# A transformer block's MLP on one core: the early pairs' evictions, splits and row steps set one sum apart

## The chip, the cores and the metric

The kernel runs on one core of a Trainium2 chip. The metric is the device time of one execution in microseconds. A core has five engines that work at once, each through its own queue in order: TensorE (PE, matrix products, into banks of PSUM), VectorE (DVE), ScalarE (ACT), GpSimd (POOL) and SyncE (SP, which here only starts transfers). SP, ACT and POOL each start DMA transfers from their queues. An engine goes on until an instruction waits for another engine's result.

## The reference, cut to what matters

One layer of a diffusion backbone: a token mixer (pooling and neighbourhood attention, one output projection), then a squared-ReLU MLP, each between two RMS norms with modulation. All tensors are 32-bit floats; 1024 tokens, width 1024, hidden width 4096. What the change touches is the end of the mixer and the start of the MLP:

```python
def _rmsnorm(x, g):
    y = x32 * lax.rsqrt(jnp.mean(x32 * x32, axis=-1, keepdims=True) + EPS)
    return (y * g.astype(jnp.float32)).astype(x.dtype)
def _modulate(x, gain, shift, scale):
    return _rmsnorm(x, gain) * (1 + scale) + shift
def _sq_relu_mlp(h, w1, w2):
    return jnp.square(jax.nn.relu(h @ w1)) @ w2
...
x = x + gt1 * _rmsnorm(mix_x, g_post_mix[l])
y_x = _sq_relu_mlp(_modulate(x, g_pre_mlp[l], sh2, sc2), w_mlp_in[l], w_mlp_out[l])
x = x + gt2 * _rmsnorm(y_x, g_post_mlp[l])
```

## The kernel before, in words

**Products.** A 32-bit product is made of three products of rounded parts: each operand is split into a high part (a copy cast to the rounded type, by ScalarE) and a low part (the operand less its high part, by VectorE), and `three` (lines 173 to 175) adds high × high, high × low and low × high. Large products are made by a scheme of seven products in place of eight: each operand is cut into four blocks, and sums of blocks are multiplied. In the MLP's first product the weights' blocks are A11, A12, A22 and the combinations S1 to S4; the tokens' blocks are B11, B21, B22 and the combinations T1 to T4. B11 and B21 come from the first 512 tokens alone.

**Pairs.** The 4096 hidden features are 16 pairs p of 256. A pair needs seven **sums**; a sum is 12 matmuls of 128 × 128 by 128 × 512 (four blocks of the inner dimension, three products each) in one PSUM bank. The first sum (A11 by B11) is copied out as s1 (`first_sum`, line 1329), the second (A12 by B21) goes on in the same bank phx and gives, with Relu and square, the hidden block r11 (`second_sum`, `squared`, lines 1276 and 1277), which is kept in DRAM (hdA11). The other five (S2 by T2 in bank phy, S1 by T1 and S4 by B22 in phz, S3 by T3 and A22 by T4 in phv) are made in `block_pair`.

**The early pairs.** The first two sums of a pair need only the first half of the tokens. So while the second half of the tokens is still on its way through the residual, the norms and the transposes, TensorE makes the first two sums of pairs 0 to EARLY − 1 (8). s1 of the first SPILLED pairs (4) goes to DRAM and is loaded again (`reload`); r11 of all early pairs is loaded again too.

**The row steps** (`row_steps`), one chain for each of the rows t = 4 to 7 (128 tokens each): `gate_steps` (ScalarE's mean square, jo; VectorE's product with the gate into mp1), `row_root` (vm on VectorE, a power on POOL, rm), `row_added` (VectorE adds the residual into xr, POOL's queue stores it as x1, ScalarE takes its mean square, sx), `row_second` (vn on VectorE, a power on POOL, rn), `row_scaled` (VectorE, into mp1). When all four are there, 32 transposes (px) and ScalarE and VectorE make the second token half (nf), `second_steps` makes T1 and T2 on VectorE and T3 and T4 by adding transfers from POOL's queue (`add_to`), and `token_part` splits ten pages (th the high, tl the low part).

**What sets the order.** Around the change the order on ScalarE and VectorE is the program's own: `in_order` ties every instruction of these engines to the one before it, from `last_product` to the end of the early pairs; TensorE's order is the program's from the projection on. After that, in pairs 1 to 14, a scheduler places VectorE's and ScalarE's work. Each call of `step` first makes the weight parts of the sum that comes four sums later (`more`: cast and subtraction, wpA11_p and wpA12_p), then the sum's matmuls. Loads of weights (wa) go through SP's queue into four buffers. The early loop is

```python
for q in both:
    xs[q], early[q] = first_sum(q)
    if q != 3:
        next(between)
for q in both:
    second_sum(q, xs[q])
    next(between, None)
```

where `between` goes through the row steps and then the second half's steps, one piece at a time.

## Time and profile before

| | us |
|---|---|
| median of 3 runs | 1062.57 |
| lowest, highest | 1061.94, 1064.35 |
| the profiled execution | 1062.89 |
| its span, first to last instruction | 1061.1 |
| mean granted TensorE clock in it | 0.992 |

A row of the time-ordered view has the start and length in us, the engine, the line of the kernel, the operation, output and inputs by the program's names without numbers, the shapes, how many equal instructions follow each other, and in brackets how long the engine was idle before it and whose result ended that. A view of waits has total, number and longest. A view by stretches has the busy time of each engine with the number of its instructions in parentheses, then the clock that TensorE was granted (1.00 is full), the mean busy share of the DMA engines and the rate.

### The profile page before, as it was taken

How to read it: one execution, taken by the hardware profiler on the slowest of the kernel's cores; microseconds unless marked ns; L12 is line 12 of the kernel's file. 1: busy time of each engine (PE TensorE's matmuls, PEld its weight loads, DVE VectorE, ACT ScalarE, POOL GpSimd, SP SyncE). 2: the span in 40 equal slices, each digit the busy share in tenths (PEclk: the TensorE clock that was granted, in tenths of full speed). 3: DMA queues.
4: the chain of work that ended last, by engine and by line, in shares of the span. 5: the costliest groups of instructions: out<-in, count | busy, mean ns of one | idle time of the engine just before them, and what ended most of it. 6: DMA issues, size and time to landing. Idle time of an engine off the chain costs nothing.

```text
span 1061.1 us, 15511 instructions
## 1 busy us (share of the span) xinstructions
PE 1037.5 (98%) x5878; PEld 853.6 (80%) x5878; DVE 709.6 (67%) x1115; ACT 531.9 (50%) x925; POOL 91.5 (9%) x145
## 2 busy tenths in 40 slices
PE   8999999999999999889999999999999999999997
PEld 7788888877888788677888888888888888888885
DVE  5535736537997598668988766665577566557586
ACT  7562021257888556766555455554563335334441
POOL 2020000051321302410000000000000000000001
PEclk9999999999999999898999999999999999999999
DMA  9905854023337776675766445345597666546556
GB/s 344 323 21 197 281 178 128 21 74 99 71 91 190 165 187 196 216 173 175 259 216 218 149 138 189 129 152 196 207 358 261 235 238 220 192 165 202 176 188 206
DMA packets 104891, 196.97 MB, mean 186 GB/s; under 512 B 8048, under 2 KB 42608, under 8 KB 104816
## 3 DMA queue, kind: packets, MB, share of 16 engines
q1 hardware_dynamic: 81888, 150.82, 43.4%
q10 hardware_dynamic: 16848, 30.44, 7.7%
q0 software_dynamic: 6080, 14.71, 6.5%
q8 instruction: 46, 0.75, 0.3%
q14 instruction: 29, 0.24, 0.1%
HBM read 147.70 MB, written 38.81 MB: 176 GB/s over the span
## 4 chain that ended last, share of the span: by engine, by line
PE 92%; ACT 4%; DVE 2%; issue 1%; DMA 1%; SPq 0%; ACTq 0%; POOL 0%; DVEq 0%; POOLq 0%
PE pk L409 4%; PE S L723 3%; PE pa L799 3%; PE pyv L174 3%; PE pyv L173 3%; PE pyz L174 3%; PE pyz L173 3%; PE pyx L174 3%; PE phv L175 3%; PE phz L175 3%; PE pyx L175 3%; PE phz L173 3%; PE phv L173 3%; PE phv L174 3%; PE phz L174 3%; PE pyx L173 3%
## 5 line engine op out<-in xcount | busy, mean ns | idle before, releaser
L173 PE MATMUL phx<-thB,wpA 128*128 128x512 f32 x128 | 52.8, 413 | 10.5 <-ACT s L1329 10.5
L1276 ACT ACTIVATE c<-c 128x512 f32<-128x512 f32 x48 | 30.3, 632 | 53.7 <-DVE c L1381 22.5
L746 ACT ACTIVATE sp<-sp,nm 128x640 f32<-128x640 f32 (+1 forms) x64 | 51.4, 803 | 9.0 <-DVE nm L737 8.7
L140 POOL TENSOR_TENSOR ry<-vy,nhalf 128x1 f32<-128x1 f32 x8 | 4.4, 549 | 584.5 <-DVE vy L138 584.5
L737 DVE CUSTOM_DVE_ANT_0 sp<-S,tab 128x640 f32<-128x640 f32 (+1 forms) x56 | 42.8, 802 | 17.9 <-PE S L723 11.4
L145 DVE TENSOR_TENSOR wpS<-S,wpS 128x512 fp32r<-128x512 f32 x64 | 43.8, 687 | 13.0 <-ACT wpS L144 13.0
L174 PE MATMUL phx<-tlB,wpA 128*128 128x512 f32 x128 | 51.9, 406 | 0.0
L175 PE MATMUL phx<-thB,wpA 128*128 128x512 f32 x128 | 51.7, 404 | 0.0
L144 ACT CAST wpS<-S 128x512 fp32r<-128x512 f32 x64 | 39.3, 615 | 23.6 <-PE phv L175 9.2
L173 PEld LDWEIGHTS phx<-thB,wpA 128*128 128x128 f32 x128 | 25.4, 198 | 17.0 <-ACT s L1329 11.8
L1277 ACT ACTIVATE c<-c 128x512 f32<-128x512 f32 x48 | 30.3, 631 | 12.8 <-DVE sa L1344 12.1
L175 PEld LDWEIGHTS phx<-thB,wpA 128*128 128x128 f32 x128 | 25.3, 198 | 5.6
L174 PEld LDWEIGHTS phx<-tlB,wpA 128*128 128x128 f32 x128 | 25.5, 199 | 5.3
L723 PE MATMUL S<-kT,q 64*128 64x384 f32 (+1 forms) x128 | 27.9, 495 | 0.4 <-DVE nm L737 0.4
L1389 DVE TENSOR_TENSOR c<-u,phz 128x512 f32<-128x512 f32 x16 | 11.0, 686 | 25.0 <-PE phz L175 25.0
L799 PE MATMUL pa<-pt,v 128*64 128x128 f32 x352 | 25.9, 280 | 0.8 <-ACT px L779 0.3
L784 DVE COPY pt<-T 128x512 f32<-128x512 f32 x32 | 21.9, 686 | 5.4 <-PE T L765 5.4
L173 PE MATMUL phy<-thT,wpS 128*128 128x512 f32 x64 | 24.9, 389 | 0.0
L174 PE MATMUL phy<-tlT,wpS 128*128 128x512 f32 x64 | 24.9, 389 | 0.0
L175 PE MATMUL phy<-thT,wpS 128*128 128x512 f32 x64 | 24.9, 389 | 0.0
L173 PE MATMUL phz<-thT,wpS 128*128 128x512 f32 x64 | 24.9, 389 | 0.0
L174 PE MATMUL phz<-tlT,wpS 128*128 128x512 f32 x64 | 24.9, 389 | 0.0
(1024 smaller groups left out, 3340.9 us busy)
## 6 DMA issues: line engine op xcount, KB each, us to landing
b<-in_w SPq DMA_DIRECT2D x64, 512.0 KB, 4.2
hrS<-hdS SPq DMA_DIRECT2D x32, 512.0 KB, 5.3
hrA<-hdA SPq DMA_DIRECT2D x24, 512.0 KB, 5.6
wm<-in_w_mod SPq DMA_DIRECT2D x16, 512.0 KB, 9.7
wa_0w<-in_w SPq DMA_DIRECT2D x16, 512.0 KB, 5.5
wa_1w<-in_w SPq DMA_DIRECT2D x16, 512.0 KB, 4.3
hdA<-c ACTq DMA_DIRECT2D x32, 256.0 KB, 2.1
hdS<-sa ACTq DMA_DIRECT2D x32, 256.0 KB, 2.6
```

The costliest lines, as they stand in the source:

```text
L144: nc.scalar.copy(hi, src)
L145: nc.vector.tensor_tensor(lo, src, hi.bitcast(F32), sub)
L173: nc.tensor.matmul(ps, ahi, bhi, start=first, stop=False, skip_group_check=more)
L174: nc.tensor.matmul(ps, ahi, blo, start=False, stop=False, skip_group_check=more)
L175: nc.tensor.matmul(ps, alo, bhi, start=False, stop=last, skip_group_check=more)
L409: nc.tensor.matmul(pks[b][j], wk(wgt, k, low, j * P, P), r, start=(k == 0 and n == 0), stop=(k == KT - 1 and n == 2))
L723: nc.tensor.matmul(S[e][:, c0 : c0 + keys.shape[1]], q[hs, cols], keys[hs], start=True, stop=True)
L737: nc.vector.tensor_tensor_reduce(out=to, in0=s, in1=bt, scale=1.0, scalar=BIG, op0=add, op1=ALU.min, accum_out=nm)
L746: nc.scalar.activation(sp, sp, AF.Exp, bias=least[i, e], scale=-1.0, accum_out=sums[i][:, e : e + 1])
L799: nc.tensor.matmul(pa[e * HD : (e + 1) * HD, cols], v[:, f : f + HD], turns[i][:, e, c] if c < 4 else fifths[i][:, :, (e + 1) * HD : (e + ...
L1276: nc.scalar.activation(r, src, AF.Relu)
L1277: nc.scalar.activation(r, r, AF.Square)
```

## The change

The early pairs become ten (EARLY 10), and six first sums go to DRAM (SPILLED 6). The early stage is now one loop over single sums, each a step, in which things are set apart in time:

- What ends a sum (`ending`: the copy of a first sum, or Relu and square of a second) is emitted at the head of the next step, before that step's weight cast.
- Of every split in the stage ScalarE's cast is emitted in its step and VectorE's subtraction in the next (`behind`, `caught_up`).
- For pairs 0 to 3 the square after the Relu moves from ScalarE to VectorE, one step later, and the transfer that keeps it two steps later.
- The row steps are cut into ten pieces instead of six, with `row_squared` (ScalarE's mean square of the added row) split off; row 7's second-half gate steps move from before the first sum to the second step.
- The transposes of the second half stand ahead of pair 5's second sum, after eleven sums of the early stage instead of eight; each of the two T combinations and each of the ten token pages has a step of its own. What is left of them after the last sum follows in one go.

Its core (`less_split` is now a case of `step_split`):

```diff
+    def step_split(src, hi, lo, less=False):
+        if less:
+            nc.scalar.activation(hi, src, AF.Copy, scale=-1.0)
+        else:
+            nc.scalar.copy(hi, src)
+        def second():
...
+        if stepwise:
+            behind.append(second)
+        else:
+            second()
...
             nc.gpsimd.dma_start(x1d[t], xt)
+            if t < 4:
+                row_squared(t)
+
+        def row_squared(t):
             root[t] = sm(f"sx_{t}", 1, 4)
-            mean_square(mp1[t], xt, root[t])
+            mean_square(mp1[t], rows[t], root[t])
...
+        def row_steps():
+            yield
             gate_steps(1, 7)
             gate_steps(0, 4)
             yield
             row_root(4)
             gate_steps(0, 5)
+            yield
+            row_added(4)
             row_root(5)
+            yield
+            row_squared(4)
+            row_added(5)
             gate_steps(0, 6)
             yield
             row_second(4)
+            row_squared(5)
             row_root(6)
             gate_steps(0, 7)
             yield
+            row_scaled(4)
             row_second(5)
+            row_added(6)
             row_root(7)
...
-            for name, src in (("T2", t2), ("T1", t1), ("T3", b12), ("B22", b22), ("T4", b21)):
+            for kp in range(2):
+                combined(kp)
+                yield
+            for name in ("T2", "T1", "T3", "B22", "T4"):
                 for kp in range(2):
-                    token_part(name, kp, src[kp])
-                yield
+                    token_part(name, kp, source[name][kp])
+                    yield
...
-        EARLY, SPILLED = 8, 4
+        EARLY, SPILLED = 10, 6
...
+        def second_kept(p, x):
+            r11 = part(f"r11_{p}")
+            if p < 4:
+                nc.scalar.activation(r11, x, AF.Relu)
+                def square():
+                    nc.vector.tensor_tensor(r11, r11, r11, mul)
+                    behind.append(lambda: keep("A11", p, r11))
+                behind.append(square)
+            else:
+                squared(x, r11)
+                defer(keep, "A11", p, r11)
+            return r11
...
+            stepwise.append(True)
+            between, xs, ending = row_steps(), {}, None
             for p in range(0, EARLY, 2):
...
+                for sum in (1, 2):
+                    for q in (p, p + 1):
+                        if ending:
+                            ending()
+                        caught_up()
+                        if (q, sum) == (5, 2):
+                            between = second_steps(*second_half())
+                        if sum == 1:
+                            xs[q] = bank(f"phx{q}")
+                        step(xs[q], "B11" if sum == 1 else "B21", sum == 1)
+                        next(between, None)
+                        if sum == 1:
+                            ending = lambda q=q: early.update({q: first_kept(q, xs[q])})
+                        else:
+                            ending = lambda q=q: second_kept(q, xs[q])
+            ending()
+            caught_up()
+            for _ in between:
+                caught_up()
+            caught_up()
+            stepwise.clear()
```

What this does to the queues, at three places. ScalarE's queue from row 5's mean square to the copy of pair 2's first sum (s1_2 from bank phx2), before:

```order
L131 ACTIVATE mp1_5_4660,sx_5_4978<-xr5_4667 128x1024
L131 ACTIVATE jo0_7_4980,ssm0_2016<-co0_7_4853 128x512
L148 ACTIVATE wpA12_3_4983<-wa3w_4911 128x512
L1276 ACTIVATE r11_1_4998<-phx1_4910 128x512
L1277 ACTIVATE r11_1_4998<-r11_1_4998 128x512
L1297 DMA hdA11_0_4677<-r11_1_4998 128x512
L131 ACTIVATE mp1_6_4819,sx_6_5012<-xr6_4669 128x1024
L144 CAST wpA11_4_5018<-wa4w_5016 128x512
L1329 COPY s1_2_5033<-phx2_5015 128x512
```

and in the change, from pair 0's Relu (r11_0) to the same copy:

```order
L1382 ACTIVATE r11_0_4954<-phx0_4884 128x512
L157 ACTIVATE wpA12_3_4958<-wa3w_4906 128x512
L1382 ACTIVATE r11_1_4978<-phx1_4905 128x512
L1339 DMA hdA11_0_4677<-r11_0_4954 128x512
L159 CAST wpA11_4_4986<-wa4w_4984 128x512
L131 ACTIVATE mp1_4_4656,sx_4_5000<-xr4_4665 128x1024
L131 ACTIVATE jo0_6_5004,ssm0_2016<-co0_6_4817 128x512
L1369 COPY s1_2_5007<-phx2_4983 128x512
```

The copy stood behind three rows' mean squares (4 to 6); it now stands behind row 4's alone, and the two squares of r11 are gone from this queue.

VectorE's queue beside it (co is the row's mixer output, vm and vn the sums under the roots), before:

```order
L149 SCALAR_TENSOR_TENSOR wpA12_2_4949<-wa2w_4887,wpA12_2_4949 128x512
L136 TENSOR_SCALAR vn_4_4968<-sx_4_4944 128x1
L138 SCALAR_TENSOR_TENSOR vm_6_4972<-ssm0_2016,ssm1_2017 128x1
L1034 SCALAR_TENSOR_TENSOR xr5_4667<-mp1_5_4660,rm_5_4940,xr5_4667 128x1024
L1013 TENSOR_TENSOR mp1_7_4884<-co0_7_4853,Ga_3853 128x512
L149 SCALAR_TENSOR_TENSOR wpA12_3_4983<-wa3w_4911,wpA12_3_4983 128x512
```

and in the change:

```order
L163 SCALAR_TENSOR_TENSOR wpA12_2_4933<-wa2w_4885,wpA12_2_4933 128x512
L1385 TENSOR_TENSOR r11_0_4954<-r11_0_4954 128x512
L1055 SCALAR_TENSOR_TENSOR xr4_4665<-mp1_4_4656,rm_4_4949,xr4_4665 128x1024
L138 SCALAR_TENSOR_TENSOR vm_5_4974<-ssm0_2016,ssm1_2017 128x1
L163 SCALAR_TENSOR_TENSOR wpA12_3_4958<-wa3w_4906,wpA12_3_4958 128x512
L1385 TENSOR_TENSOR r11_1_4978<-r11_1_4978 128x512
```

The subtraction of pair 3's A12 stood behind row 5's residual and follows row 4's now; each Relu's square has its place after a subtraction.

ScalarE's queue at the end of the early stage, from the Relu of the last early pair to the copy of pair 0's z, before:

```order
L1276 ACTIVATE r11_7_5372<-phx7_5309 128x512
L1277 ACTIVATE r11_7_5372<-r11_7_5372 128x512
L1297 DMA hdA11_3_4680<-r11_7_5372 128x512
L148 ACTIVATE wpA22_0_5382<-wa0_1w_5279 128x512
L144 CAST wpS2_1_5407<-S2_1_5405 128x512
L1376 COPY c22_0_5422<-phz0_5398 128x512
```

and in the change:

```order
L1318 ACTIVATE r11_9_5440<-phx9_5375 128x512
L1319 ACTIVATE r11_9_5440<-r11_9_5440 128x512
L1339 DMA hdA11_4_4681<-r11_9_5440 128x512
L159 CAST thB22_1_5446<-nf1_3_5222 128x1024
L159 CAST thT4_0_5450<-nf0_2_4857 128x1024
L159 CAST thT4_1_5454<-nf0_3_4877 128x1024
L157 ACTIVATE wpA22_0_5464<-wa0_1w_5349 128x512
L1433 COPY c22_0_5504<-phz0_5480 128x512
```

Three token pages now stand after the last early sum, where none did.

## The prediction

> **What bounds the kernel now.** First the page's list of engines: TensorE is busy almost all the time, so only its idle and slow stretches are to be won.

> ```profile
> PE 1037.5 (98%) x5878; PEld 853.6 (80%) x5878; DVE 709.6 (67%) x1115; ACT 531.9 (50%) x925; POOL 91.5 (9%) x145
> ```

> Then busy time by stretches (columns: stretch and length in us, then PE, PEld, DVE, ACT, POOL busy with instruction counts, granted PE clock, DMA share, GB/s):

> ```profile
> 300.00:400.00 100.00, 99.50 (x927) 81.21 (x926) 75.71 (x167) 67.30 (x153) 17.88 (x20) 1.00 0.70 171
> 400.00:500.00 100.00, 89.51 (x401) 73.58 (x401) 74.09 (x105) 68.23 (x116) 20.44 (x24) 0.93 0.63 187
> 500.00:600.00 100.00, 100.00 (x443) 82.81 (x442) 85.97 (x137) 53.53 (x92) 0.00 (x0) 1.00 0.66 222
> 423.24:487.23 63.99, 53.50 (x227) 43.38 (x226) 44.66 (x60) 46.21 (x77) 14.70 (x16) 0.89 0.62 178
> ```

> One stretch of the three is both idle and at a lower clock, and the change is in it: 423.24 to 487.23 us is the stage of the early pairs, from the first matmul of pair 0's first sum to the first of pair 0's T2 sum. Who TensorE waited for, 400 to 520 us (total, times, longest):

> ```profile
> PE phx L173 <- ACT s L1329: 10.5, 3, 5.6
> ```

> Each time it is ScalarE's copy of a finished first sum (s, line 1329), without which the second sum may not go on in that bank. TensorE in order of time:

> ```profile
> 423.24 0.47 PE L173 MATMUL phx<-thB,wpA 128*128 128x512 f32 x1
> ...
> 429.36 0.50 PE L173 MATMUL phx<-thB,wpA 128*128 128x512 f32 x1 [0.39 <-ACT s L1329]
> ...
> 440.14 0.39 PE L175 MATMUL phx<-thB,wpA 128*128 128x512 f32 x1
> 445.03 0.80 PE L173 MATMUL phx<-thB,wpA 128*128 128x512 f32 x1 [4.50 <-ACT s L1329]
> 445.62 0.63 PE L174 MATMUL phx<-tlB,wpA 128*128 128x512 f32 x1
> ...
> 450.74 0.40 PE L174 MATMUL phx<-tlB,wpA 128*128 128x512 f32 x1
> ...
> 453.28 3.65 PE L1120 MATMUL px<-ident,mp 128*128 128x128 f32 x32
> 456.69 0.48 PE L173 MATMUL phx<-thB,wpA 128*128 128x512 f32 x1
> ...
> 478.87 0.79 PE L173 MATMUL phx<-thB,wpA 128*128 128x512 f32 x1 [5.60 <-ACT s L1329]
> ...
> 484.95 0.40 PE L175 MATMUL phx<-thB,wpA 128*128 128x512 f32 x1
> ...
> 487.23 0.39 PE L173 MATMUL phy<-thT,wpS 128*128 128x512 f32 x1
> ...
> 500.83 0.39 PE L173 MATMUL phy<-thT,wpS 128*128 128x512 f32 x1
> ```

> After each long wait a matmul takes 0.63 us, not 0.39, for some 6 us; after the short one it doesn't. The granted clock (last column but two) says why:

> ```profile
> 440.00:445.00 5.00, 0.53 (x3) 0.11 (x1) 3.16 (x6) 4.00 (x9) 2.70 (x3) 0.89 0.91 294
> 445.00:450.00 5.00, 4.97 (x12) 3.95 (x13) 3.12 (x6) 2.77 (x5) 1.99 (x2) 0.50 1.01 384
> 480.00:485.00 5.00, 5.00 (x14) 3.89 (x13) 5.00 (x6) 3.60 (x5) 0.00 (x0) 0.51 0.17 52
> ```

> Why is ScalarE late? Its own queue before the first wait, the second and the third, and one row of VectorE's:

> ```profile
> 427.60 0.63 ACT L131 ACTIVATE jo<-co 128x512 f32<-128x512 f32 x1
> ...
> 428.73 0.57 ACT L1329 COPY s<-phx 128x512 f32<-128x512 f32 x1
> 429.34 0.33 ACTq L1331 DMA_DIRECT2D s<-s  x1
> ...
> 438.47 1.06 ACT L131 ACTIVATE mp<-xr 128x1024 f32<-128x1024 f32 x1 [0.94 <-DVE xr L1034]
> ...
> 441.26 0.63 ACT L1277 ACTIVATE r<-r 128x512 f32<-128x512 f32 x1
> ...
> 442.84 1.06 ACT L131 ACTIVATE mp<-xr 128x1024 f32<-128x1024 f32 x1 [0.94 <-DVE xr L1034]
> 443.89 0.60 ACT L144 CAST wpA<-wa4w 128x512 fp32r<-128x512 f32 x1
> 444.40 0.58 ACT L1329 COPY s<-phx 128x512 f32<-128x512 f32 x1
> ...
> 472.91 1.99 ACT L144 CAST thT<-nf 128x1024 fp32r<-128x1024 f32 x2 [0.73 <-ACT r L1277]
> 477.71 0.62 ACT L144 CAST wpS<-S 128x512 fp32r<-128x512 f32 x1 [2.81 <-DVE S L1249]
> 478.24 0.58 ACT L1329 COPY s<-phx 128x512 f32<-128x512 f32 x1
> ```

> ```profile
> 440.79 0.69 DVE L149 SCALAR_TENSOR_TENSOR wpA<-wa3w,wpA 128x512 fp32r<-128x512 f32 x1 [1.75 <-ACT wpA L148]
> ```

> The second copy (444.40) stands behind row 6's mean square (442.84), which waits for VectorE's row 6; that row stands behind VectorE's split of a weight (440.79), which waits 1.75 us for ScalarE's cast, which itself stands behind row 5's mean square. So each row is one round between the engines, 442.84 − 438.47 = 4.37 us long, while TensorE does a sum in 2.7 (below). The third copy stands behind a cast that waits 2.81 us for VectorE, which is still splitting token pages. Neither engine is full (46.21 and 44.66 us busy of 63.99): they wait in turn.

> **What the change can win.** From the rows: 487.23 to 500.83 is five sums, so a sum takes 13.60 / 5 = 2.72 us. The 32 transposes take 456.69 − 453.28 = 3.41. Sixteen sums and the transposes would be 43.52 + 3.41 = 46.93 us; they take 63.99, so **17.06 us** are lost. Parts: waits 0.39 + 4.50 + 5.60 = 10.49; the low clock, 445.03 to 450.74 for 13 matmuls that take 13 × 0.227 (13.60 / 60) = 2.95 elsewhere, 2.76, and 478.87 to 484.95 for 14 (3.17), 2.91; the other 0.9 is restarts and odd rows.

> [...]

> **The change part by part.** *Pairs 8 and 9 become early:* four sums move from pairs 8 and 9 into the stage, 4 × 2.72 = 10.88 us, at the same price if TensorE doesn't wait: 0. Their A11 and A12 weights are now loaded apart, ahead of pair 0's on SP's queue, and two sums more go to DRAM and back. The slowest such load of the stage:

> ```profile
> wa7w<-in_w SPq DMA_DIRECT2D x1, 512.0 KB, 6.1
> ```

> Pair 8's load finds its buffer free when pair 4's A12 is split, in the eighth sum, and is cast in the thirteenth: 13.6 us for 6.1. Pair 0's own loads follow pairs 6 and 7 in the same way, and with a DMA share of 0.62 the queues have room: 0. Without that cover the price would be one TensorE wait as long as the lateness.

> *Evictions one sum later, second halves of splits one sum later:* a sum's copy or Relu is now the first thing that ScalarE does in the next sum's step, and VectorE's subtraction follows a step behind its cast, so neither waits for the other within a step. Weights are still cast four sums ahead (10.9 us), so the lag of 2.72 is covered. The copy itself now waits for TensorE at the head of a step; queued behind it are a cast wanted 10.9 us later and a row step, so nobody near waits for that wait. The second sum of a pair comes two sums after the first: the copy has 2.72 us, less its own 0.58. All three old waits go by this: the first because row 7's mean square (427.60, 0.63) now stands behind pair 0's copy, which needed only 0.39; the second and third because no copy has a row or an S cast of its own step ahead of it.

> *Squares of pairs 0 to 3 move to VectorE:* 4 × 0.63 leave ScalarE (441.26), 4 × 0.69 come to VectorE (a two-operand row as 440.79). VectorE had 44.66; with 2.8 for the squares and 2.8 for four more weight splits it has 50.2 of 57.8, 87%: 0, hidden under TensorE; without that cover, 2.8. The DMA that keeps a square leaves a sum later still; its reader comes with its block pair, over 20 us on.

> *Row steps and transposes:* the transposes now stand behind eleven sums, 29.9 us after the first matmul. The old chain, with all its waits, had row 7 scaled at 452.33, 29.1 us after it (the row below). Spread over ten steps with fewer waits it should be earlier; VectorE's answers from POOL are the loose end:

> ```profile
> 451.58 0.75 DVE L1043 TENSOR_SCALAR mp<-xr,rn 128x1024 f32<-128x1024 f32 x1 [0.45 <-POOL rn L140]
> ```

> I take 0.3 us, between 0 and 2.

> *Token combinations, one page a step:* ScalarE is the fuller engine now. In the stage it had 46.21; minus 2.52 for the squares, plus two pairs' copies and Relus (4 × 0.58), squares (2 × 0.63) and casts (4 × 0.60) makes 49.7; 16 DMA issues of 0.33 (429.34, not counted as busy), 0.35 with the next start, make 5.6. That is 55.3 us of a stage of 20 × 2.72 + 3.41 = 57.8, 96%. But B22's second page and both of T4 (3 × 1.0) and one weight (0.6) may come after its end: B22 is wanted 3 and T4 4 sums later. After pair 9's last sum ScalarE does Relu, square and issue (1.6), three pages (3.0), a cast and the copy of z (1.2): 5.8, and the B22 sum needs that copy 8.2 after. So it may be 2.4 late without harm. I expect about that, and waits of 0.8 in all around B22 and T4. Bounds: 0; and 3, which would be one wait shorter than any here that lowered the clock.

> The accumulating transfers on which T3 and T4 hang land as late as

> ```profile
> nf<-nf POOLq DMA_DIRECT2D x2, 512.0 KB, 6.1
> nf<-t POOLq DMA_DIRECT2D x2, 512.0 KB, 8.6
> ```

> after the issue. They are issued from the twelfth to the fourteenth sum, and the first page that needs one is cast five sums (13.6 us) on: 0.

> **Sum:** −17.06 + 0.3 + 0.8 = −16.0 us. Against the profiled execution: span 1061.1 − 16.0 = 1045.1, its time 1062.9 − 16.0 = 1046.9. The median of the three runs, 1062.57, stands 0.3 lower: **1046.6 us**. Without any new wait it would be 1062.6 − 17.1 = 1045.5, with both bounds (2 and 3) 1050.5: that is the forecast's own range.

> **Rivals.**
> *One: ScalarE becomes the bound.* Of its 17.8 us of idle in the old stage 12 issues are 4.2 and true waits 13.6. If these all stay, it needs 55.3 − 3.6 + 13.6 = 65.3 for a stage of 57.8. From 1 us beyond the 2.4 spare it decides; 7.5 late in one long wait, with 2.8 of low clock, is 10.3: 1045.5 + 10.3 = **1055.8**. For it: the 96%. Against: its longest waits were mp on xr (0.94 a row) and the cast on S (2.81), and between the two ends of each a step now lies.

> *Two: VectorE blocks POOL.* POOL's rsqrt rows differ while VectorE runs a long row:

> ```profile
> 438.83 0.61 POOL L140 TENSOR_TENSOR rm<-vm,nhalf 128x1 f32<-128x1 f32 x1
> 441.70 1.81 POOL L140 TENSOR_TENSOR rn<-vn,nhalf 128x1 f32<-128x1 f32 x1 [1.73 <-DVE vm L138]
> 441.52 1.28 DVE L1034 SCALAR_TENSOR_TENSOR xr<-mp,rm,xr 128x1024 f32<-128x1024 f32 x1
> ```

> If each of the eight POOL steps also meets one of the new VectorE squares, 8 × 0.69 = 5.5 us come onto the row chain; 29.1 + 5.5 is 4.7 after 29.9, a TensorE wait at the transposes, with 2.8 of low clock 7.5: 1045.5 + 7.5 = **1053.0**. Against: four squares can't meet eight steps, and four rows overlap each other. [...]

> *Three: the loss moves into the block pairs.* VectorE is 86% busy from 500 to 600, so it catches up 1.9 us in a pair's 13.6; it had 5.6 us to run ahead while TensorE waited at 473, and these are gone. What pair 0 can't make up, 5.6 − 1.9 = 3.7, would be a wait in pair 1, with 2.8 of low clock 6.5: **1052.0**. For it: the steps leave T4 and pair 1's weights to the last moment. Against: VectorE's 87% in the stage leave it 7 us in hand, spread over the steps.

> *Four, slower:* the steps are a lock: if every step still holds one handover of 0.94 us (as mp on xr) on ScalarE, a step costs 55.3 / 20 + 0.94 = 3.7 us, 1.0 above 2.72, and twenty steps lose 20, more than the 17.06 won: **1065.5**. From 2.72 + 17.06 / 20 = 3.57 us a step it is slower. Against: a copy or Relu that waits for TensorE alone finds the sum of the step before done.

> *Five: nothing changes,* because another engine holds TensorE at the same places: 1062.6. Against: the three waits have one releaser.

> **How the numbers follow.** Forecast 0.70, rival one 0.10, two 0.04, three 0.10, four 0.03, five 0.03. The range 1045.0 to 1053.5 holds the forecast, two and three, and the milder part of one; its lower end lies 0.5 below the case without any wait, for the median's own spread. A measurement here tells 0.2% (2.1 us) from no change: faster is the forecast and rivals one to three, 0.94; same 0.03; slower 0.03.

> **What would show it.** Right: in 423 to 490 us no TensorE wait over 1 us and no granted clock of 0.50; phy's first matmul 57.8 to 59.5 us after phx's first; ScalarE's copies start within 3 us of a sum's end; ten phx copies there. Row 7 scaled before 453. Wrong: a wait at px (rows late: two), at phz or phv of pair 0 over 3 us (one), TensorE idle in 500 to 530 (three), small waits at every sum (four).

## The result: 1046.57 us, as forecast

| | before | after |
|---|---|---|
| median of 4 executions, us | 1062.37 | 1046.57 |
| lowest, highest | 1061.94, 1064.35 | 1046.48, 1049.19 |
| ratio, 95% interval | | 0.9854, 0.9834 to 0.9873 |

The kernel is 1.5% faster. The execution that was profiled is the 1049.19: it reaches the early stage 2.1 us later (425.35 against 423.24), in instructions that are the same in both kernels, and a second profile below (run 1) does not show that.

The stretches of the changed kernel that answer to the old ones; the last is its early stage, from the first phx matmul to the first phy matmul, now with twenty sums (columns as before: stretch, length, busy time of PE, PEld, DVE, ACT and POOL, granted clock, DMA share, GB/s):

```profile
400.00:500.00 100.00, 100.00 (x470) 82.69 (x469) 79.47 (x113) 71.34 (x122) 20.39 (x25) 0.95 0.70 210
500.00:600.00 100.00, 100.00 (x443) 82.78 (x442) 90.94 (x147) 55.65 (x95) 0.00 (x0) 0.95 0.73 244
425.35:483.78 58.43, 58.43 (x275) 48.51 (x273) 44.61 (x63) 45.41 (x79) 13.73 (x16) 0.95 0.80 230
```

By its busy column TensorE is never idle in the stage (58.43 of 58.43). The 0.95 is one figure that stands over this whole execution; the stretch from 300 to 400 us has it too (0.95, where the second profile has 1.00). TensorE in order of time:

```profile
425.35 0.48 PE L194 MATMUL phx<-thB,wpA 128*128 128x512 f32 x1
...
455.47 3.75 PE L1145 MATMUL px<-ident,mp 128*128 128x128 f32 x32
...
483.78 0.39 PE L194 MATMUL phy<-thT,wpS 128*128 128x512 f32 x1
...
492.10 0.50 PE L194 MATMUL phz<-thB,wpS 128*128 128x512 f32 x1
...
495.14 0.50 PE L194 MATMUL phv<-thT,wpA 128*128 128x512 f32 x1
...
497.99 0.39 PE L194 MATMUL phy<-thT,wpS 128*128 128x512 f32 x1
```

The stage takes 483.78 − 425.35 = 58.43 us where 20 × 2.72 + 3.41 = 57.81 is the least. Pair 0's five sums take 497.99 − 483.78 = 14.21 in place of 13.60: the B22 sum (492.10) and the T4 sum (495.14) each begin with a longer first matmul, 0.50, after a wait too short for the list of waits. For equal work, the old stage with four sums more and a pair (63.99 + 10.88 + 13.60 = 88.47) stands against 58.43 + 14.21 = 72.64: **15.8 us won**. After that nothing differs: from the first matmul of pair 1 to the end of the span it is 1047.4 − 497.99 = 549.4 now and 1061.1 − 500.83 − 10.88 = 549.4 before.

### The profile page after: what moved, and what is told of

The parts are those of the page before. It is cut to its first block, busy times and chain, and to the rows that moved or that the text cites. A ratio compares the mean times of both kernels' runs of the same rounds, so it can differ in the third digit from the quotient of the medians.

```text
span 1047.4 us, 15539 instructions
## 1 busy us (share of the span) xinstructions
PE 1033.6 (99%) x5878; PEld 850.1 (81%) x5878; DVE 710.8 (68%) x1119; ACT 530.1 (51%) x921; POOL 90.5 (9%) x145
## 4 chain that ended last, share of the span: by engine, by line
PE 95%; DMA 2%; ACT 1%; DVE 1%; issue 0%; SPq 0%; DVEq 0%; POOLq 0%; ACTq 0%
PE pk L430 4%; PE S L744 4%; PE pa L820 4%; PE phz L194 3%; PE phv L194 3%; PE phx L194 3%; PE phx L195 3%; PE phz L195 3%; PE pyv L196 3%; PE phv L195 3%; PE phx L196 3%; PE pyv L194 3%; PE pyz L196 3%; PE pyz L194 3%; PE pyx L194 3%; PE pyx L195 3%
## 5 line engine op out<-in xcount | busy, mean ns | idle before, releaser
L140 POOL TENSOR_TENSOR ry<-vy,nhalf 128x1 f32<-128x1 f32 x8 | 4.4, 549 | 570.9 <-DVE vy L138 570.9
L194 PE MATMUL phx<-thB,wpA 128*128 128x512 f32 x128 | 50.1, 392 | 0.0
L196 PE MATMUL phx<-thB,wpA 128*128 128x512 f32 x128 | 49.9, 390 | 0.0
L1319 ACT ACTIVATE c<-c 128x512 f32<-128x512 f32 x48 | 30.3, 631 | 14.4 <-DVE sa L1401 13.6
L194 PEld LDWEIGHTS phx<-thB,wpA 128*128 128x128 f32 x128 | 24.0, 188 | 5.4 <-ACT s L1369 0.4
L196 PEld LDWEIGHTS phx<-thB,wpA 128*128 128x128 f32 x128 | 24.0, 188 | 5.1
L194 PE MATMUL phz<-thB,wpS 128*128 128x512 f32 x64 | 25.0, 391 | 0.0
L194 PE MATMUL phv<-thT,wpA 128*128 128x512 f32 x64 | 25.0, 391 | 0.0
L195 PE MATMUL phz<-tlB,wpS 128*128 128x512 f32 x64 | 24.9, 390 | 0.0
L195 PE MATMUL phv<-tlT,wpA 128*128 128x512 f32 x64 | 24.9, 389 | 0.0
L196 PE MATMUL phz<-thB,wpS 128*128 128x512 f32 x64 | 24.9, 389 | 0.0
L194 PE MATMUL phy<-thT,wpS 128*128 128x512 f32 x64 | 24.9, 389 | 0.0
## 6 DMA issues: line engine op xcount, KB each, us to landing
b<-in_w SPq DMA_DIRECT2D x64, 512.0 KB, 4.2
hrS<-hdS SPq DMA_DIRECT2D x32, 512.0 KB, 5.3
hrA<-hdA SPq DMA_DIRECT2D x24, 512.0 KB, 5.6
wm<-in_w_mod SPq DMA_DIRECT2D x16, 512.0 KB, 9.7
wa_0w<-in_w SPq DMA_DIRECT2D x16, 512.0 KB, 5.0
wa_1w<-in_w SPq DMA_DIRECT2D x16, 512.0 KB, 4.3
```

The costliest lines, as they stand in the source:

```text
L194: nc.tensor.matmul(ps, ahi, bhi, start=first, stop=False, skip_group_check=more)
L195: nc.tensor.matmul(ps, ahi, blo, start=False, stop=False, skip_group_check=more)
L196: nc.tensor.matmul(ps, alo, bhi, start=False, stop=last, skip_group_check=more)
L1319: nc.scalar.activation(r, r, AF.Square)
```

## The experiments

Two theories are set against each other in most runs. *Of the queues*: TensorE waited because a copy or a cast stood in a queue behind pieces of work longer than the 2.72 us of a sum, so order and size of the pieces decide. *Of the load*: ScalarE and VectorE had too much to do, so only the amount of work in the stage decides. The runs come in three groups, each beside runs of the kernel before on the same chip (medians 1061.66, 1061.86 and 1062.21).

### 1. The changed kernel once more

No edit.

> The changed kernel once more, unedited. The profile taken of it lost 2.1 us ahead of the early stage, in instructions that are the same in both kernels. If that was this one execution: median 1046.5, within 0.5; first phx matmul at 423.2 within 0.5; stage (first phx to first phy of pair 0) 58.4 within 0.4. If the change itself slows what comes before: first phx again at 425 or later.

Measured: 1046.58 (1046.53 to 1046.85), ratio 0.9854 (0.9838 to 0.9871). Its early stage, and ScalarE's queue around the copy of pair 2's first sum, for which TensorE waited 4.50 us before:

```profile
423.11:481.41 58.30, 58.30 (x275) 48.38 (x274) 44.63 (x63) 45.32 (x79) 13.73 (x16) 1.00 0.80 230
```

```profile
435.44 1.06 ACT L131 ACTIVATE mp<-xr 128x1024 f32<-128x1024 f32 x1
...
436.49 0.62 ACT L131 ACTIVATE jo<-co 128x512 f32<-128x512 f32 x1
...
437.16 0.59 ACT L1369 COPY s<-phx 128x512 f32<-128x512 f32 x1
...
438.79 0.62 ACT L159 CAST wpA<-wa5w 128x512 fp32r<-128x512 f32 x1 [1.04 <-DVE xr L1055]
```

The stage begins at 423.11, so the 2.1 us were of that one execution. The clock is full throughout (1.00). The fifth sum's successor starts at 436.96, and the fifth sum's copy 0.2 us later (437.16), although a row's mean square (435.44) stands ahead of it: the row's residual was there, since it was a step older. ScalarE still idles here (1.04 behind VectorE's residual), but at a cast that nobody wants for 10.9 us.

### 2. Eight early pairs again

```diff
-        EARLY, SPILLED = 10, 6
+        EARLY, SPILLED = 8, 4
```

> Eight early pairs again (four first sums to DRAM), all else as in the change. The stage has 16 sums: 16 x 2.72 + 3.41 = 46.9 us, 11 less than with ten pairs. From the twelfth sum on five of the twelve token pieces have a step of their own, so seven pages stand behind the last early sum in place of three. Theory of the queues: on ScalarE Relu, square and issue 1.6, seven pages 7.0, a cast and the copy of z 1.2 make 9.8 us after the last sum, and the B22 sum wants that copy at 8.2; VectorE's seven low parts (7 x 1.2) come beside pair 0's own work. So waits of 2 to 4 us in all in pair 0 at phz and phv, each under 3.4 us and without a low clock: 1048.5 to 1050.5. Rival of the load (only the work of ScalarE and VectorE per time counts): the same work over 2.72 x 4 = 10.9 us less of TensorE in the stage, but pair 0 to 2 have room: 0, 1046.5. Rival that the two pairs are what wins: eight pairs fall back by 8 us or more, 1054.5.

Measured: 1050.21 (1050.06 to 1050.78), 3.6 us slower than the change, where the queues' theory had 1048.5 to 1050.5. All waits of TensorE from 415 to 530 us (total, times, longest):

```profile
PE phz L194 <- ACT c L1433: 1.3, 1, 1.3
PE phv L194 <- DVE c L1437: 0.8, 1, 0.8
PE phz L195 <- DVE tlT L165: 0.8, 1, 0.8
```

The queues' theory holds: pair 0 takes 17.93 us in place of 14.21, and the stage itself, 47.3 us, is nearly as short as it can be (46.9). The load's theory (no change) falls, and so does the rival by which the two pairs are worth 8 us. So the two further pairs win nothing by themselves; they give four steps more in which token pages come one at a time.

### 3. The copy in its own step

```diff
                         step(xs[q], "B11" if sum == 1 else "B21", sum == 1)
-                        next(between, None)
                         if sum == 1:
                             ending = lambda q=q: early.update({q: first_kept(q, xs[q])})
                         else:
                             ending = lambda q=q: second_kept(q, xs[q])
-            ending()
+                        ending()
+                        ending = None
+                        next(between, None)
```

> The change, but what ends a sum is put into the queues right behind the sum's own step (cast, copy, row or token piece) in place of the head of the next. The amount of work is the same. Theory of the queues: a piece of the rows or tokens now stands behind the copy of its own step, which waits for TensorE, and so starts up to a sum (2.72 us) later than before; in the rows the slack to the transposes is 0.2 us, and behind the last sum one more token page is left (four x 1.0 in place of three). Expected: waits of 2 to 4 us around the ninth pair's first sum or at px, and 3 to 4 us at B22 of pair 0, 5 to 9 us in all: 1051.5 to 1055.5. Rival of the load: same work, same time, 1046.5 within 0.5.

Measured: 1052.80 (1052.49 to 1053.25), 6.2 us slower than the change. The waits from 415 to 530 us:

```profile
PE phz L194 <- ACT c L1433: 3.1, 1, 3.1
PE phx L194 <- ACT s L1369: 1.5, 1, 1.5
```

Both are where they were expected, the second (1.5) shorter than the 2 to 4 us of the expectation; px is not late. With the copies back in their old place, the first two waits of the kernel before (0.39 and 4.50) do not come back: no other phx waits. The remaining 1.6 us or so are a stretch of half clock after the 3.1 us wait (0.50 from 494.68 to 498.09 us), to which run 8 comes back. The load's theory (no change) falls.

### 4. The row steps in the old, larger pieces

The ten pieces of `row_steps` are cut as before, but row 7's second-half gate steps stay in the stage (the first pieces shown):

```diff
         def row_steps():
-            yield
             gate_steps(1, 7)
             gate_steps(0, 4)
             yield
             row_root(4)
             gate_steps(0, 5)
-            yield
-            row_added(4)
             row_root(5)
-            yield
+            row_added(4)
             row_squared(4)
-            row_added(5)
             gate_steps(0, 6)
             yield
...
```

> The change, but the row steps are cut as before it (six pieces; a row's residual and its mean square in one piece; row 7's second-half gate step stays in the early stage). The amount of work is the same, and the transposes stand at the same place. Theory of the queues: each of the first copies stands behind a piece with a whole round to VectorE; a round took 4.37 us and a sum 2.72, so the copies of three rows come 4.37 - 2.72 = 1.65 us late each, and the first, behind two gate squares more (0.39 + 0.63), 1.0: about 6.0 us, in waits of 1 to 3.4 us in the first three pairs, 1052.5 (1050 to 1056 as one of them lowers the clock or not). Rival of the load: 1046.5 within 0.5. Rival of the split handover (the lag of the splits did it all): 1046.5 too, since the lag stays.

Measured: 1053.74 (1053.68 to 1053.82), 7.2 us slower than the change. TensorE in order of time, and the stretches around the second wait:

```profile
430.28 0.50 PE L194 MATMUL phx<-thB,wpA 128*128 128x512 f32 x1 [1.00 <-ACT s L1364]
...
435.79 0.50 PE L194 MATMUL phx<-thB,wpA 128*128 128x512 f32 x1 [2.45 <-ACT s L1364]
...
446.37 0.50 PE L194 MATMUL phx<-thB,wpA 128*128 128x512 f32 x1 [0.48 <-ACT s L1364]
```

```profile
433.63:437.05 3.42, 1.26 (x6) 1.05 (x6) 2.95 (x6) 3.02 (x7) 2.58 (x4) 1.00 0.51 205
437.05:440.46 3.41, 3.41 (x10) 2.64 (x9) 2.30 (x6) 2.42 (x6) 1.12 (x3) 0.50 0.69 210
```

The copies of pairs 0, 1 and 2 are late, as expected, but by 3.9 us in all and not by 6.0. The expectation left open whether one of the waits lowers the clock; that of 2.45 us did (0.50 in the second stretch), so the total lies in the forecast range with a third less of waiting and some 1.6 us of half clock (an estimate, worked out in the last section). The subtractions still lag here, so the lag alone does not do it. The same amount of work in larger pieces costs nearly half of the change's gain.

### 5. The kernel before with the late copy alone

```diff
...
+                        if ending:
+                            ending()
+                        more()
+                        product(xs[q], ready.pop(0), "B11" if sum == 1 else "B21", sum == 1)
...
+                        if (q, sum) != (3, 1):
+                            next(between, None)
```

> The kernel before with one part of the change alone: what ends a sum is put at the head of the next step, ahead of that step's weight cast. Row pieces, splits, squares, token pages and the eight pairs stay as before. Rival that the place of the copies is what wins (no copy stands behind the cast of its own step): the third wait, behind the cast that waited 2.81 us for VectorE, goes, with its low clock 5.60 + 2.91 = 8.5: 1054. Theory of the queues: with the old large pieces the copy of a sum now stands behind the row piece of its own step, a round to VectorE of 4.37 us against the sum's 2.72, in the first five steps; the first waits of before (0.39 and 4.50) get one piece longer (about 1 and 4.37 more) and one more appears at the second pair: 3 to 10 us slower than before, 1065 to 1072. Rival of the load: 1062, the same.

Measured: 1070.05 (1068.87 to 1070.52), ratio to the kernel before 1.0070 (1.0055 to 1.0085): slower by 8.2 us. The waits from 415 to 530 us, and ScalarE's queue before the longest:

```profile
PE phx L173 <- ACT s L1327: 15.5, 5, 6.0
```

```profile
451.02 1.06 ACT L131 ACTIVATE mp<-xr 128x1024 f32<-128x1024 f32 x1 [2.02 <-DVE xr L1034]
...
452.07 0.57 ACT L1327 COPY s<-phx 128x512 f32<-128x512 f32 x1
```

There were three waits and 10.5 us; there are five and 15.5 (1.00, 3.40, 6.03, 2.64 and 2.45). The last stands where the third of before, 5.60, was: it is shorter but not gone, which it would be by the rival of the copies' place. A copy at the head of the next step stands behind the whole row piece of its own step, which with the old pieces holds a round to VectorE (2.02 us of idle ahead of the mean square, which then takes 1.06). The same edit that is worth 6.2 us inside the change (run 3) costs 8.2 without its other parts.

### 6. The kernel before with the late subtraction alone

```diff
-                (less_split if n in ("A12", "A22") else split)(src, blocks(w[:, :512]), blocks(w[:, 512:]))
+                step_split(src, blocks(w[:, :512]), blocks(w[:, 512:]), n in ("A12", "A22"))
...
                 for q in both:
+                    caught_up()
                     xs[q], early[q] = first_sum(q)
```

> The kernel before with another part alone: VectorE's subtraction of a split comes one step after ScalarE's cast; all else as before. Rival of the handover (the round between the engines inside a step is the cause): the second and third wait go, with their low clock, 4.50 + 2.76 + 5.60 + 2.91 = 15.8: 1046. Theory of the queues: a row's residual no longer waits 1.75 us for a cast, and the S cast no longer stands as long behind token pages, so each of the two waits gets 1 to 1.75 us shorter, to 2.8 to 3.5 and 3.9 to 4.6; the row pieces before the copies and the two pages a step remain: 2 to 5 us faster than before, 1057 to 1060 (the lower end if one of the waits then costs one window of low clock less).

Measured: 1059.16 (1058.02 to 1059.59), ratio 0.9971 (0.9958 to 0.9984): 2.7 us faster than before. The waits from 415 to 530 us:

```profile
PE phx L197 <- ACT s L1353: 7.8, 3, 4.1
```

The three waits are 0.39, 3.32 and 4.09 us, where they were 0.39, 4.50 and 5.60. The handover within a step was 10.49 − 7.8 = 2.7 us of the waiting and not the heart of it: the rival falls. (In the profiled execution the matmuls of 0.63 us after the second wait run from 444.19 to 446.75 us, one half-clock stretch, where before they run from 445.62 to 450.74, two; the medians don't show what that is worth.)

### 7. Two token pages in a step

```diff
             for kp in range(2):
                 combined(kp)
-                yield
+            yield
             for name in ("T2", "T1", "T3", "B22", "T4"):
                 for kp in range(2):
                     token_part(name, kp, source[name][kp])
-                    yield
+                yield
```

> The change, but both token combinations in one step and both pages of a token operand in one step, as before it (five steps less; no page is left behind the last sum). Same work. Theory of the queues: a step with two pages gives ScalarE 2 x 1.0 + a cast 0.60 + a copy 0.58 + an issue 0.35 (every other step) = 3.4 and VectorE 2 x 1.2 + 0.6 and a block combination = 3.6, both over a sum's 2.72; over five such steps 3.5 to 4.5 us of lateness, which comes out in one wait at a phx of pairs 8 or 9; with one or two windows of low clock (1.6 each) 5 to 8 us in the stage. Pair 0's waits of 0.6 go, since no page is left: 1050.5 to 1054. Rival of the load: the same work, and pair 0 without its waits: 1046.0.

Measured: 1052.49 (1051.73 to 1053.07), 5.9 us slower than the change. ScalarE ahead of pair 8's copy, and TensorE behind it:

```profile
476.69 0.62 ACT L159 CAST wpS<-S 128x512 fp32r<-128x512 f32 x1 [1.64 <-DVE S L1291]
477.21 1.99 ACT L159 CAST thT<-nf 128x1024 fp32r<-128x1024 f32 x2
479.10 0.58 ACT L1369 COPY s<-phx 128x512 f32<-128x512 f32 x1
```

```profile
479.73 0.50 PE L194 MATMUL phx<-thB,wpA 128*128 128x512 f32 x1 [4.18 <-ACT s L1369]
```

This is the third wait of the kernel before, two pairs later (pair 8's copy in place of pair 6's): an S cast that waits for VectorE, and pages in pairs ahead of a copy. That the last pages are done in time doesn't help; one long wait takes it back.

### 8. The clock by itself

```diff
             c22 = part(f"c22_{p}")
+            for _ in range({2: 3, 3: 5, 4: 4, 5: 6, 6: 5, 7: 8, 8: 4, 9: 5, 10: 9, 11: 12, 12: 10, 13: 13, 14: 10}.get(p, 0)):
+                nc.scalar.copy(c22, z)
             nc.scalar.copy(c22, z)
```

> The change with 3 to 13 further copies of z into c22 ahead of the copy of c22 in pairs 2 to 14 (3, 5, 4, 6, 5, 8, 4, 5, 9, 12, 10, 13, 10 of them; 0.52 us each): TensorE has to wait for the last before the B22 sum. The result stays the same. Some thirteen waits, of 1 to 6.5 us, at least 13 us apart. The run with large row pieces showed half clock for 3.4 us after waits of 1.00 and 2.45 us; the run with the copy in its own step for 3.4 us after 3.09; the kernel before for 6.8 after 4.50 and 5.60. Theory of the windows: the clock is set anew every 3.41 us on a fixed grid by TensorE's busy share in the stretch before: at 0.37 or less it halves, at 0.46 or more it stays, and while halved a stretch with 0.76 busy keeps it there and a full one ends it. Then waits of 2.1 to 3.4 us halve it or not by their place on the grid, all above 4.0 halve it, low stretches last 3.4 or 6.8 us (never 4 or 5), and each costs about 1.6 per 3.4 us. Rival of the length (as in the prediction): only waits over 3.1 us or so halve it, whatever their place, and each costs 2.8.

Measured: 1103.76 (one execution). TensorE's waits from 500 to 900 us, and stretches of 3.41 us on the grid on which the clock changes in this trace (busy PE is the first of the engines, the clock the last but two):

```profile
PE phz L194 <- ACT c L1435: 37.3, 13, 5.2
```

```profile
549.05:552.46 3.41, 1.60 (x7) 1.05 (x6) 2.08 (x4) 2.53 (x5) 0.00 (x0) 1.00 0.64 207
552.46:555.87 3.41, 3.41 (x9) 2.64 (x9) 1.29 (x3) 1.26 (x2) 0.00 (x0) 0.50 0.61 226
566.12:569.53 3.41, 1.52 (x7) 0.94 (x5) 1.86 (x3) 2.84 (x7) 0.00 (x0) 1.00 0.65 210
569.53:572.94 3.41, 2.25 (x10) 1.86 (x11) 1.60 (x3) 1.86 (x4) 0.00 (x0) 1.00 0.53 189
...
586.60:590.01 3.41, 2.98 (x7) 2.40 (x8) 1.49 (x3) 1.64 (x3) 0.00 (x0) 0.50 0.44 160
590.01:593.42 3.41, 3.41 (x16) 2.83 (x16) 1.94 (x3) 1.85 (x3) 0.00 (x0) 1.00 0.20 77
...
685.58:689.00 3.42, 1.64 (x4) 1.35 (x5) 2.67 (x4) 1.70 (x4) 0.00 (x0) 0.50 0.17 64
689.00:692.41 3.41, 3.41 (x10) 2.64 (x9) 0.00 (x0) 1.26 (x2) 0.00 (x0) 0.50 0.20 77
```

A wait of 1.81 us, which lies wholly in the first of these stretches, is followed by half clock in the next (0.50 at 552.46); one of 3.04, spread over the third and fourth, is not (1.00 at 569.53). So length alone does not decide. A half-clock stretch with 2.98 of 3.41 busy (586.60) is followed by full clock (1.00 at 590.01), one with 1.64 (685.58) by a second at half clock (0.50 at 689.00). Of the thirteen waits nine were followed by half clock, for eleven stretches in all. The time agrees: 37.3 of waits and half of the 34 us that TensorE was busy in those eleven stretches, 17, make 54.3; measured are 1103.76 − 1046.57 = 57.2. The 2.9 between, 0.2 a wait, are restarts by the author's estimate (the first matmul after a wait takes 0.50 us, as at 518.48, where the others take 0.39). The theory of the windows holds in this run, that of the length falls. One bound of the expectation was off: a stretch with 0.46 or more busy was to leave the clock alone, and 1.60 of 3.41 is 0.47.

### 9. The squares back on ScalarE

```diff
-            if p < 4:
+            if p < 0:
                 nc.scalar.activation(r11, x, AF.Relu)
```

> The change with the squares of pairs 0 to 3 back on ScalarE (4 x 0.63 us more there, 4 x 0.69 less on VectorE). Theory of the queues: a square stands behind its own sum's Relu and ahead of a cast that is wanted four sums later; a step's queue still fits in 2.72 us after one or two steps, so at most one small wait: 0 to 0.7 us, 1046.6 to 1047.3. Rival one of the prediction (ScalarE's load is the bound, 96% of the stage): 2.5 us come on top of all later work, and the copy of z comes that much later: a wait of 2.5 or more at B22 of pair 0, 1049 or more. Rival two (VectorE's long rows hold POOL back): without the squares row 7 is scaled up to 2.8 us earlier than now (29.3 us after the first phx matmul), with nothing won, since the transposes stand behind eleven sums anyway.

Measured: 1047.20 (1047.18 to 1047.63), 0.6 us slower than the change, within the queues' 0 to 0.7; the ratios don't tell the two apart (0.9846 to 0.9879 here, 0.9834 to 0.9873 for the change). No wait of TensorE is listed. Row 7's scaling on VectorE, in the change (run 1) and here:

```profile
451.62 0.75 DVE L1068 TENSOR_SCALAR mp<-xr,rn 128x1024 f32<-128x1024 f32 x1
```

```profile
452.12 0.75 DVE L1068 TENSOR_SCALAR mp<-xr,rn 128x1024 f32<-128x1024 f32 x1
```

From the first phx matmul (423.11 and 423.02) to its end that is 29.3 us in the change and 29.9 here: without the squares on VectorE the row chain is later, not earlier. The last seven of POOL's eight power steps do take longer beside the squares, 7.19 us in run 1 against 5.88 here, but that is 1.3 us and not the 5.5 of rival two, and before the change they took 8.86. Rivals one and two of the prediction both fall by this run.

### 10. The subtraction in the cast's step

```diff
-        if stepwise:
-            behind.append(second)
-        else:
-            second()
+        second()
```

> The change with VectorE's subtraction of a split in the same step as ScalarE's cast. Theory of the queues: the row chain gets some rounds more; row 7 is now scaled 0.7 us before the transposes could start, and four subtractions that wait 0.4 to 0.5 us each for their cast make 1.8: a wait of 0.8 to 1.6 us at px, and a token page's second half no worse than now: 1047.3 to 1048.3. Rival of the handover (the lag is the heart of the change): 5 us or more, 1051.5. Rival that it is worth nothing: 1046.6.

Measured: 1049.17 (1049.07 to 1049.88), 2.6 us slower than the change, where 0.8 to 1.6 were expected. TensorE at the transposes:

```profile
454.19 0.64 PE L1142 MATMUL px<-ident,mp 128*128 128x128 f32 x3
456.56 3.38 PE L1142 MATMUL px<-ident,mp 128*128 128x128 f32 x29 [1.73 <-DVE mp L1065]
```

The place is right, the wait is 1.73, and the px matmuls also start 0.35 us later than in run 1 (counted from the first phx matmul, 423.67 here); with a restart of 0.2, as estimated in run 8, that is 2.3 of the 2.6. The estimate had taken four subtractions with 0.4 to 0.5 us of waiting each; it was too small. No phx wait is listed. As in run 6 the lag is worth 2.6 to 2.7 us.

### 11. Twelve early pairs

```diff
-        EARLY, SPILLED = 10, 6
+        EARLY, SPILLED = 12, 8
```

> Twelve early pairs, eight first sums to DRAM, all else as in the change: four steps more behind the transposes, so no page is left behind the last sum. Theory of the queues: the two small waits of pair 0 (0.16 and 0.32, with their restarts 0.6 us) go: 1046.0, within 0.3. If the further transfers or the weights loaded apart cost something: 1046.6 or more.

Measured: 1046.56 (1045.79 to 1046.81), ratio 0.9854 (0.9839 to 0.9869): no difference from the change that can be told. In its profile pair 0's five sums run from 491.89 to 505.49, 13.60 again, so its 0.6 us are gone, as expected; but only the profiled execution, the fastest, is faster by them. No version was found that beats the change by more than the noise.

### 12. The transposes earlier

```diff
-                        if (q, sum) == (5, 2):
+                        if (q, sum) == (5, 1):
+                            for _ in between:
+                                pass
                             between = second_steps(*second_half())
```

> The change with the transposes one sum earlier (behind ten sums; the row steps still open come first). Theory of the queues: row 7 is scaled 29.3 us after the first phx matmul and ten sums end at 27.2, so a wait of about 2 us at px (1.6 to 2.1); the token pages come one step earlier and pair 0's 0.6 go: +1.3, 1047.9. By the rule of the windows a wait of 2 us halves the clock only if nearly all of it falls into one stretch of 3.41 us (busy share 0.46 or less): then 1.7 more, 1049.6. Rival that the place of the transposes gives the win away (earlier is better): 1046.0 or less.

The expectation misread the loop: pair 5's first sum is the tenth, so the transposes stood behind nine sums, two fewer than in the change. Measured: 1050.42 (four executions: 1049.48, 1049.72, 1051.12, 1052.67; mean clock 0.998, 0.998, 0.997, 0.995), 3.8 us slower than the change, so the rival (earlier is better) falls. TensorE at the transposes in the profiled execution (1052.67), and the stretches there:

```profile
450.12 0.33 PE L1145 MATMUL px<-ident,mp 128*128 128x128 f32 x1 [1.70 <-DVE vn L136]
451.66 6.29 PE L1145 MATMUL px<-ident,mp 128*128 128x128 f32 x29 [1.22 <-DVE mp L1068]
```

```profile
447.42:450.83 3.41, 1.33 (x7) 0.73 (x5) 2.25 (x6) 1.34 (x3) 1.85 (x3) 1.00 1.09 365
450.83:454.24 3.41, 2.58 (x12) 2.58 (x13) 1.56 (x2) 1.13 (x2) 0.00 (x0) 0.50 0.97 319
454.24:457.66 3.42, 3.42 (x18) 3.42 (x17) 2.82 (x3) 2.34 (x4) 0.42 (x1) 0.50 0.00 1
```

The rows are late by 1.70 + 1.22 = 2.9 us, and this execution pays two stretches of half clock for it. The other three times lie 1.55, 2.95 and 3.19 us below; two or one stretch fewer, at an estimated 1.6 each, would give 1049.5 and 1051.1, and their mean clocks go the same way. That the waits were the same in those three is likely but not shown, as only one execution has a trace.

## Why the prediction was right, and where it was not

**The loss and its cause** stood as forecast. The three waits are gone, the stage's granted clock is full in run 1 (1.00), its ten copies start at most 2.1 us after their sums, and the gain for equal work is 15.8 us against 16.0. The cause, copies and casts queued behind too large pieces, is what runs 3, 4, 5 and 7 show from four sides, all with the same amount of work: moving a copy by one piece costs 6.2, larger row pieces 7.2, larger token pieces 5.9, and the copies' new place without the smaller pieces 8.2 us. In none of these runs did the load decide.

**The parts do not add up.** Undone one at a time they cost 3.6, 6.2, 7.2, 5.9, 0.6 and 2.6 us, 26.1 in all, more than the 15.8 that they win together (the transposes' old place, after eight sums, was not tried). Of the two tried alone on the kernel before one wins 2.7 and one loses 8.2.

**Evictions and lag, "all three old waits go by this":** wrong, though the three waits are gone. The prediction's reason for the second and third, that "no copy has a row or an S cast of its own step ahead of it", is not what the queue does. Emitted at the head of the next step, a copy stands behind the cast and the row or token piece of its own step: pair 2's copy behind row 4's mean square (437.16 and 435.44 in run 1), and pair 8's behind an S cast that waits and a token page:

```profile
473.73 0.62 ACT L159 CAST wpS<-S 128x512 fp32r<-128x512 f32 x1 [1.46 <-DVE S L1291]
474.26 1.05 ACT L159 CAST thT<-t 128x1024 fp32r<-128x1024 f32 x1
475.22 0.57 ACT L1369 COPY s<-phx 128x512 f32<-128x512 f32 x1
```

Pair 8's first sum ends at 473.1 and its second begins at 475.84, so this copy comes just in time. What took the waits away is, in the main, that the row and token pieces are smaller. With the copies in their old place (run 3) or without the lag (run 10) the first two waits do not come back; with the larger row pieces waits at the first copies do (run 4), and with two pages in a step the third does (run 7). The prediction gave these pieces no part of the 17.06 us; that the sum came out right all the same is luck in this point. Only its answer to rival one (between the two ends of each wait "a step now lies") came near: pair 8's S cast still waits 1.46 us, but no copy is late by it. The late copy is worth its 6.2 us elsewhere: the rows and pages no longer wait behind a copy that waits for TensorE.

**Pairs 8 and 9, 0:** right. From pair 1 on the time is the same 549.4 us, and twelve pairs cost nothing either.

**Squares, 0:** right as far as can be told. On ScalarE they would cost some 0.6 us, which the intervals don't separate from nothing.

**Row steps and transposes, +0.3:** the size was right by luck. In run 1 the transposes start 453.29 − 423.11 = 30.18 us after the first phx matmul, 0.26 later than eleven sums; but row 7 is scaled 0.9 us before that, so the rows, for which the 0.3 stood, cost nothing. The 0.26 are small delays of the sums themselves, such as a first matmul of 0.45 at 428.68. The sentence that the new row chain "should be earlier" than the old 29.1 us was wrong: it ends after 29.3, and "row 7 scaled before 453" holds in run 1 (452.4) and fails in the first profile (454.4, with 2.1 us of start). One piece a step paces it: in run 12, where the last pieces are not spread, it ends at 450.85 + 0.75 − 423.32 = 28.3. What covered it is the place of the transposes, eleven sums, which left 0.9 us in run 1.

**Token pages, +0.8:** 0.6, and the working was close. ScalarE at the end of the stage in run 1:

```profile
484.09 0.59 ACT L1318 ACTIVATE r<-phx 128x512 f32<-128x512 f32 x1
...
486.73 2.00 ACT L159 CAST thT<-nf 128x1024 fp32r<-128x1024 f32 x2
...
489.15 0.57 ACT L1433 COPY c<-phz 128x512 f32<-128x512 f32 x1
```

The Relu of the last sum comes 484.09 − 481.41 = 2.7 us late (forecast about 2.4), and the copy of z ends 8.3 us after the stage; it was wanted at 8.2. The upper bound of 3 us rested on the sentence that such a wait is "shorter than any here that lowered the clock". Run 8 shows the clock halved after 1.81, so that bound should have been 3 + 1.6 = 4.6. Run 2 is that bound's case: its three waits (0.76, 1.27 and 0.76, 2.8 us in all) cost no clock (1.00 from 475 to 488 us). That waits under 3.4 us leave the clock alone, as run 2's expectation has it, no run shows; 1.81 us was enough in run 8.

**Low clock, 2.76 and 2.91 a time:** right for these two waits, but not a constant, as the prediction's rivals used it. The kernel before, in stretches of its own grid of 3.41 us:

```profile
440.51:443.92 3.41, 0.02 (x1) 0.00 (x0) 2.68 (x5) 2.44 (x6) 2.22 (x3) 1.00 0.88 293
443.92:447.33 3.41, 2.30 (x6) 1.84 (x7) 2.61 (x4) 1.88 (x4) 2.37 (x3) 0.50 1.03 354
447.33:450.74 3.41, 3.41 (x9) 2.67 (x8) 1.72 (x4) 2.13 (x6) 0.22 (x2) 0.50 0.81 323
```

The wait of 4.50 us reached 1.1 us into the next stretch, which then had 2.30 of 3.41 busy, and the one after it was at half clock too (0.50 at 447.33); so it cost two stretches, where the wait of 4.18 in run 7 cost one. Runs 3, 4 and 7 show a single half-clock stretch after a wait (494.68 to 498.09 us in run 3, 437.05 to 440.46 in run 4, both with 3.41 of 3.41 busy; matmuls of 0.63 us from 480.56 to 483.55 in run 7).

**The rivals.** One fell by run 9. The prediction's 96% for ScalarE also counts the pages and the weight that come after the stage; in run 1 ScalarE is busy for 45.32 of 58.30 us, which with 14 issues of some 0.4 us makes 51 at most, or 87%. Two fell by run 9: POOL's steps are longer beside the squares by 1.3 us, in place of 5.5. Three fell by the equal 549.4 us, though VectorE is busier there (90.94 of 100 against 85.97). Four fell by the stage without listed waits. Five fell by the result.

## What to carry to other kernels

Before shifting work between engines, write down for each queue what stands ahead of the one instruction that the busiest engine wants next, and cut it into pieces that fit, together with what is wanted, into that engine's step; the same work in other pieces was worth 6 to 8 us here. A single part of such a schedule can lose alone what it wins with the others, so it is tried with them. Price a wait of the matrix engine by where it may fall on the clock's grid, not by its length alone: in run 8 half clock came after one of 1.81 us and not after one of 3.04.

## What the runs showed of the hardware

The shares are those of the kernel before and of stretches around waits in runs 3, 4, 8 and 12 (in the first trace of the change the clock is recorded as one figure). Full clock was followed by half after a share of 0.42 or less (1.42 of 3.41 at 583.18 us in run 8 is the largest of these) and went on after 0.49 or more (1.66 of 3.41 at 1051.49 us in the kernel before is the smallest). Between 0.45 and 0.48 it went either way in run 8: the 1.60 at 549.05 and at 620.73 were followed by half clock, the 1.52 at 566.12, the 1.58 at 637.80 and the 1.64 at 661.69 weren't; the ends of matmuls are modelled, so such shares are not sharp. A half-clock stretch with a share of up to 0.76 (2.59 of 3.41 at 478.05 us in the kernel before) was followed by another, one with 0.87 (2.98 at 586.60 us in run 8) and those busy throughout by full clock. A wait cost 0, 1 or 2 such stretches accordingly (in run 8 that of 3.04 us none, that of 1.81 one, that of 4.56 two). A fully busy one costs about 1.6 us, as an estimate: eight 128x512 matmuls fit in at 0.427 us apart, as in run 4, and at 0.227 they would take 1.8 of the 3.41. Waits of 2.43 us were followed by half clock twice in run 8 (they end at 534.84 and 587.03 us) and once weren't (641.81).

Counted from the first instruction, the grid does not lie the same in every profile: half-clock stretches begin at 443.92 us in the kernel before and at 494.68 in run 3, which is 14.9 stretches apart, no whole number. So a wait that leaves a stretch about half busy may cost a half-clock stretch in one execution and none in the next, which is the likely reason, not a shown one, that run 12's four executions spread over 3.2 us, and four of the change in run 1 over 0.3. It does not follow that every long wait makes a kernel vary: run 4's four, with a wait of 2.45 us, lie within 0.14.
